# Two more matrix products of a hybrid decoder block as seven block products each

## The chip, the cores and the metric

The kernel runs on one core of one Trainium2 chip. The metric is the device time of one launch in microseconds. A core has a matrix engine (TensorE, "PE" in the profile; its weight loads are "PEld"), a vector engine (VectorE, "DVE"), an activation engine (ScalarE, "ACT"), a general engine (GpSimd, "POOL") and a queue engine (SyncE, "SP") that issues most of the transfers. Each engine executes its own instructions strictly in order. Operands lie in SBUF, results of PE in PSUM (eight banks of 128x512 float32).

## What is computed

One layer, for 1024 positions of width 1024, all in float32:

```python
u  = rmsnorm(h) ;  P = u @ W_in        # [gate_a | gate_s | B_a | C_a | v_a | z | xBC | dt]
y_a = (b_a * causal_dwconv(c_a * v_a, conv_a_w)) @ w_a_out            # 1024x1024 @ 1024x1024
y   = ssd_chunked_scan(...) + d_skip * xh                             # 32 heads, chunks of 128
y_s = gated_group_rmsnorm(y, z, ssd_norm_w) @ w_s_out                 # 1024x2048 @ 2048x1024
# gated_group_rmsnorm: y*silu(z), divided by the root mean square over groups of 512, times the weight
h  = h + (sigmoid(gate_a) * y_a + sigmoid(gate_s) * y_s) @ w_o
v  = rmsnorm(h)
h  = h + (silu(causal_dwconv(v @ W_1) + b) * (v @ W_3)) @ w_down      # d_ff 2816
out = rmsnorm(h)
```

## The kernel before

**Float32 products.** Every large product is made from rounded parts: a float32 tile is split into a high part (`act.copy` to float32r) and a low part (`split`, value minus high part, on DVE or POOL). A product of a 512x128 weight block and a 512x512 operand block is 12 matmuls with 512 moving columns: high x high, high x low and low x high, for four k-blocks each (`product`). In what follows "a product" is such a dozen.

**Seven block products.** The input projection, W_1 and W_3 already use seven products of half-size blocks where eight would be needed (the Strassen-Winograd form, class `Pair`): sums of operand blocks (`a11, a12, s1, s2, s4, s3, a22`) are formed and split once, sums of weight blocks per output pair. w_down does so too, with its weight sums (`w_sums`, a tensor `td` in DRAM) prepared beforehand. y_a, w_s_out and w_o are plain products.

**Order of the work.** (1) Input projection; beside it, from a counter of products (`tick`), the 32 SSD chunks (4 groups x 8) advance in steps at fixed offsets from the chunk's place, which are 6 products apart (`STAGES`, `ssd_chunk`). The last steps of a chunk multiply y by silu(z) (tile `zt`, 2 buffers), square it, store it to DRAM (`yd`, on ACT's queue), and get 1/rms of the 128 positions by a matmul with ones (`pn`), a multiply-add on DVE and a power on POOL; after every fourth chunk these are transposed (`pr`) and stored as a row (`rd`). (2) The y_a and w_s_out stage, for each half of the positions (`ta_half`, `y_a`, `y_half`, `s_out`): operands come from DRAM (`tad`, `yd`), y is multiplied by the norm weight and the row `rd` on DVE and split; for each of eight 128-wide output columns the weights are loaded, split (low part on DVE and POOL in turn) and multiplied, in both halves again. Outputs are gated on DVE; y_a's go through DRAM (`mad`). w_down's weight sums are made beside this stage, one k-block per output column. Then w_o (`out_proj`), for four row tiles at once in the first half and two in the second, with k-blocks 0 to 3 from the first four output columns and 4 to 7 from the others. (3) The MLP: 22 pairs of seven products, with the causal convolution and gating of each pair on ACT and DVE (`ffn_done`), sums of the gated result for w_down (`g_sums`), side tiles from a pool of two (`side`). (4) w_down in four sweeps, and the final norm.

A scheduler orders each engine's instructions before the run, by the program's order as priority and a simulated timeline; tiles come from pools with a fixed number of buffers (14 `big` ones of 128x2048, 4 `x` ones of the same size that exist only after the SSD, 13 weight parts `w`, 4 `raw` weight tiles), and whatever has no free buffer waits.

Of the kernel before, what the change touches and what calls it, by code (L numbers as in the profile page):

```python
# [8 lines left out]
F32 = mybir.dt.float32  # L9
# [44 lines left out]
STAGES = LOAD_M, LOAD_IN, DECAY, TRANS, LOAD_Z, DIAG, SQUARES, NORM = -9, -9, -6, -4, -3, 0, 3, 6  # L54
# [11 lines left out]
def tile_block(  # L66
# [633 lines left out]
    states, decayed, stats = {}, {}, {}  # L700

    def ssd_chunk(s):
# [104 lines left out]
        act.dma_start(yd[g, c // 4][:, :, hts], zt)  # L807
# [6 lines left out]
        rs = tiny(f"yss{nm}")  # L814
        dve.tensor_scalar(rs, pn, 1.0 / HALF, EPS, op0=ALU.mult, op1=ALU.add)
        if c % 4 == 0:
            stats[g, c // 4] = tiny(f"yr{nm}", 4)
        r = stats[g, c // 4]
        pool.tensor_tensor(r[:, c % 4 : c % 4 + 1], rs, nhalf, op=ALU.pow)
        if c % 4 == 3:  # L820

            pr = sd_tile(f"pr{nm}")[:4, :P]
            pe.transpose(pr, r, ident)
# [45 lines left out]
    def w_sums(k):  # L869

        r, r2 = (s4(f"wd{f}{k}")[:, :SEQ] for f in range(2))
        for f, t in enumerate((r, r2)):
            sp.dma_start(t, w_down[f * KF + k])
        b11, b12 = (r[:, h] for h in halves)
        b21, b22 = (r2[:, h] for h in halves)
        sub(b11, b12, b11)
        sub(b12, b22, b12, pool)
        sub(b22, b22, b11)
        sub(b21, b22, b21, pool)
        for i, t in enumerate((b11, b22, b12, b21)):  # L880
# [3 lines left out]
    def ta_half(hf, res):
        for q in range(2):
            new = extra_tile if hf and q else big_tile
            hi, lo = new(f"tah{hf}{q}", F32R), new(f"tal{hf}{q}", F32R)
            res.append((hi, lo))
            tt = (extra_tile if hf else big_tile)(f"ta{hf}{q}")
            for k in range(0, 4, 2):  # L890
                ks = slice(k, k + 2)
                sp.dma_start(tt[:, ks, :], tad[:, 4 * q + k : 4 * q + k + 2, halves[hf]])
                split(tt[:, ks, :], hi[:, ks, :], lo[:, ks, :], dve)
                yield

    def y_a(hf, ta, beside):
        sl = halves[hf]
        for j in range(NK):
            raw = load(w_a_out[j], f"wa{hf}{j}")
            ps = mm_tile(f"ya{hf}{j}")  # L900
            for q in range(2):
                w = wsplit(raw[:, halves[q]], f"wa{hf}{j}{q}", pool if q else dve)
                product(ps, ta[q], w, start=q == 0, stop=q == 1)
            gh = c2(f"ga{hf}{j}")
            sp.dma_start(gh, gad[:, j, sl])

            dve.scalar_tensor_tensor(gh, gh, 1.0, ps, op0=ALU.add, op1=ALU.mult)
            sp.dma_start(mad[:, j, sl], gh)
            beside(j)
# [448 lines left out]
```

## Time and profile before

| | |
|---|---|
| median of 3 runs | 1973.02 us (1971.64 to 1974.24) |
| profiled execution | 1974.46 us, span of its instructions 1972.7 us, granted clock 0.989 |
| PE, PEld | 1914.5 us busy (97%), 1572.0 (80%) |
| DVE, ACT, POOL | 1289.6 us (65%), 962.0 (49%), 1236.3 (63%) |
| chain that ended last | PE 80%, DVE 7%, ACT 4% |
| HBM | 247.34 MB read, 89.41 MB written |

The profile is one execution, taken by the hardware profiler. A row of groups reads: source line, engine, operation, output tile <- input tiles, shapes, count | busy us, mean ns of one | idle time before them and what ended it. A row of windows gives, for a stretch of the span, the busy time of each engine with its instruction count, then PE's granted clock, the share of the transfer engines and GB/s. A row of the chain of waits is start, duration, what. A row of the timeline is start, duration, engine, line, operation. An operation's duration includes time in which it is held up after its start. A matmul's own row says 389 ns, but matmuls overlap; their distance is read from the chain. Names: `ya` and `so` are the PSUM tiles of y_a and w_s_out, `l_x` and `h_x` low and high parts of a weight.

### The profile page before, as it was taken

How to read it: one execution, taken by the hardware profiler on the slowest of the kernel's cores; microseconds unless marked ns; L12 is line 12 of the kernel's file. 1: busy time of each engine (PE TensorE's matmuls, PEld its weight loads, DVE VectorE, ACT ScalarE, POOL GpSimd, SP SyncE). 2: the span in 40 equal slices, each digit the busy share in tenths (PEclk: the TensorE clock that was granted, in tenths of full speed). 3: DMA queues.
4: the chain of work that ended last, by engine and by line, in shares of the span. 5: the costliest groups of instructions: out<-in, count | busy, mean ns of one | idle time of the engine just before them, and what ended most of it. 6: DMA issues, size and time to landing. Idle time of an engine off the chain costs nothing.

```text
span 1972.7 us, 25409 instructions
## 1 busy us (share of the span) xinstructions
PE 1914.5 (97%) x8986; PEld 1572.0 (80%) x8986; DVE 1289.6 (65%) x1429; ACT 962.0 (49%) x1636; POOL 1236.3 (63%) x915
## 2 busy tenths in 40 slices
PE   7899999999999999999999999998999999999998
PEld 6678887787788778888888888876888888878886
DVE  8655567767776777777664833479854655585555
ACT  6345457677546664443542323354344444453334
POOL 6657776866776776676445533458876787845342
PEclk9899999999999999999999999998999999999999
DMA  4133355545445554443998974451323344487653
GB/s 166 54 111 121 122 164 172 162 150 190 155 133 164 164 164 124 146 157 110 382 376 279 356 250 161 161 170 35 136 80 108 101 150 163 139 285 264 206 188 143
DMA packets 180175, 338.42 MB, mean 172 GB/s; under 512 B 15280, under 2 KB 87760, under 8 KB 179024
## 3 DMA queue, kind: packets, MB, share of 16 engines
q1 hardware_dynamic: 93264, 253.95, 37.7%
q10 hardware_dynamic: 86784, 82.85, 13.1%
q8 instruction: 70, 1.15, 0.2%
q14 instruction: 57, 0.47, 0.1%
HBM read 247.34 MB, written 89.41 MB: 171 GB/s over the span
## 4 chain that ended last, share of the span: by engine, by line
PE 80%; DVE 7%; ACT 4%; issue 3%; DMA 3%; POOL 2%; ACTq 1%; SPq 0%; POOLq 0%; DVEq 0%
PE pb11up L268 10%; PE so L268 9%; PE pt1up L268 6%; PE pb11xb L268 5%; PE ya L268 4%; PE pb11cv L268 4%; PE d L1151 3%; PE d L1153 3%; PE d L1152 3%; PE pb11z L268 3%; PE pb21up L268 3%; PE pb11ba L268 2%; PE pt1cv L268 2%; PE pt1xb L268 2%; DMA m<-acd 2%
## 5 line engine op out<-in xcount | busy, mean ns | idle before, releaser
L608 DVE SCALAR_TENSOR_TENSOR cv<-xbc,scw,cv 128x1024 f32<-128x1024 f32 x72 | 122.6, 1704 | 46.3 <-ACT cv L604 45.0
L608 DVE SCALAR_TENSOR_TENSOR h<-fci,fcw,h 128x1024 f32<-128x1024 f32 x44 | 85.9, 1953 | 74.1 <-ACT h L604 73.3
L724 ACT ACTIVATE m<-m,tk 128x128 f32<-128x128 f32 x256 | 79.1, 390 | 95.3 <-DMA m<-acd 91.4
L149 POOL TENSOR_TENSOR l_ws<-raw_ws,h_ws 128x512 fp32r<-128x512 f32 x32 | 46.3, 1447 | 71.1 <-PE so L268 40.8
L148 ACT CAST h_ws<-raw_ws 128x512 fp32r<-128x512 f32 x64 | 39.9, 623 | 96.8 <-PE so L268 69.3
L268 PE MATMUL so<-yh,h_ws 128*128 128x512 f32 x256 | 69.0, 391 | 0.0
L268 PE MATMUL so<-yl,h_ws 128*128 128x512 f32 x256 | 68.6, 389 | 0.0
L268 PE MATMUL so<-yh,l_ws 128*128 128x512 f32 x256 | 68.5, 389 | 0.0
L148 ACT CAST h_wo<-raw_wo 128x512 fp32r<-128x512 f32 x48 | 29.7, 621 | 60.3 <-PE wo L985 32.7
L808 DVE TENSOR_TENSOR eb<-eb 128x256 f32<-128x256 f32 x32 | 28.1, 879 | 45.6 <-ACT eb L806 45.6
L149 DVE TENSOR_TENSOR l_ws<-raw_ws,h_ws 128x512 fp32r<-128x512 f32 x32 | 25.1, 785 | 50.0 <-PE so L268 25.5
L149 POOL TENSOR_TENSOR l_wo<-raw_wo,h_wo 128x512 fp32r<-128x512 f32 x24 | 32.3, 1346 | 39.1 <-PE wo L985 30.7
L268 PEld LDWEIGHTS so<-yh,l_ws 128*128 128x128 f32 x256 | 48.0, 188 | 10.0
L268 PEld LDWEIGHTS so<-yl,h_ws 128*128 128x128 f32 x256 | 48.0, 188 | 10.0
L268 PEld LDWEIGHTS so<-yh,h_ws 128*128 128x128 f32 x256 | 47.8, 188 | 9.7
L1128 DVE TENSOR_TENSOR h<-h 128x1024 f32<-128x1024 f32 x22 | 48.7, 2212 | 9.8 <-ACT h L1127 9.6
L314 DVE TENSOR_TENSOR fci<-fci,pb21up 128x512 f32<-128x512 f32 x18 | 12.4, 688 | 60.3 <-PE pb21up L268 60.3
L149 POOL TENSOR_TENSOR l_t3up<-raw_2up,h_t3up 128x512 fp32r<-128x512 f32 x22 | 30.3, 1376 | 32.7 <-PE pb11up L268 32.7
L984 PE MATMUL wo<-l_wo,mh 128*128 128x512 f32 x128 | 50.0, 391 | 0.0
L983 PE MATMUL wo<-h_wo,mh 128*128 128x512 f32 x128 | 49.9, 391 | 0.0
L985 PE MATMUL wo<-h_wo,ml 128*128 128x512 f32 x128 | 49.7, 391 | 0.0
L1127 ACT ACTIVATE h<-h 128x1024 f32<-128x1024 f32 x22 | 23.4, 1062 | 52.7 <-DVE h L608 52.7
(1125 smaller groups left out, 6571.8 us busy)
## 6 DMA issues: line engine op xcount, KB each, us to landing
m<-acd ACTq DMA_DIRECT2D x32, 512.0 KB, 3.9
raw_ws<-in_w_s_out SPq DMA_DIRECT2D x32, 512.0 KB, 4.7
ssd_in<-cv ACTq DMA_DIRECT2D x24, 512.0 KB, 3.1
in<-ssd_in ACTq DMA_DIRECT2D x32, 384.0 KB, 3.8
raw_wo<-in_w_o SPq DMA_DIRECT2D x24, 512.0 KB, 3.8
wd<-in_w_down SPq DMA_DIRECT2D x22, 512.0 KB, 7.0
td<-wd SPq DMA_DIRECT2D x44, 256.0 KB, 4.3
raw_2up<-in_w_up SPq DMA_DIRECT2D x22, 512.0 KB, 3.4
```

The lines of the kernel that those rows point to most:

```text
L148: act.copy(hi, v)
L149: (eng or pool).tensor_tensor(lo, v, f32(hi), op=ALU.subtract)
L268: pe.matmul(ps, wt[:, k, :], ct[:, k, :], start=(start and n == 0), stop=(stop and n == 11), skip_group_check=held,)
L608: dve.scalar_tensor_tensor(cv, ci[:, j : j + SEQ], w[:, j : j + 1], cv, op0=ALU.mult, op1=ALU.add)
L724: act.activation(m[:, h, :], m[:, h, :], AF.Relu, bias=a)
L983: pe.matmul(pss[t], mh, wh, start=k == 0, stop=False)
L984: pe.matmul(pss[t], mh, wl, start=False, stop=False)
L985: pe.matmul(pss[t], ml, wh, start=False, stop=k == NK - 1)
L1128: dve.tensor_tensor(cv, cv, h3, op=ALU.mult)
L1151: pe.matmul(ps, aa[0][:, ts], bb[0], start=k == 0, stop=False)
L1152: pe.matmul(ps, aa[0][:, ts], bb[1], start=False, stop=False)
L1153: pe.matmul(ps, aa[1][:, ts], bb[0], start=False, stop=k == KF - 1)
```

## The change

y_a and w_s_out are computed by one new function, `strassen`, over all 1024 positions and all 1024 output columns at once: the operand in four blocks (half of the positions x half of the k), the weights in four blocks, seven products per output column of the half (y_a 7x4x1 products of 12 matmuls, w_s_out 7x4x2). The sums over products are kept in PSUM banks across stages (`b1`, `b2`: four banks each) with two copies in SBUF (`x1`, `x2`).

- Operand sums are formed two stages ahead (`form`): blocks loaded from DRAM, sums on POOL in pieces of 128x1024, high part on ACT, low part on DVE. They use `big` tiles.
- Weight sums (`sums`) are made on DVE when a stage needs them. y_a's four weight blocks are loaded once and held; w_s_out's are loaded per stage, and two kinds of sums (stages s1, s2) are stored to DRAM and loaded again by later stages. All low parts of weights in these stages are on POOL.
- Outputs are finished in stages a12, s4 (first half of the positions) and s3, a22 (second half). w_o of the first half runs between s4 and s3; the norm and transposes of the first four row tiles run beside s3 and a22.
- y is normalised inside `ssd_chunk`: the 1/rms of 128 positions is put on a diagonal (DVE), multiplied by ones on PE (`pr`, now 128x128, every chunk), and y is scaled by it and the weight in four DVE operations, then stored. The row `rd`, its loads and the multiplications in `y_half` go. The steps are moved: `STAGES` has z's load one product later, the norm one earlier, and a new step SCALE at 7.
- w_down's weight sums (`w_sums`) move into `g_sums`, one k-block beside each of the first 11 pairs of the MLP, after that pair's gating, all four differences on DVE, with `side` tiles.
- `load_x` takes `big` tiles for the first half; `out_proj` finds the merged tiles by half.

```diff
-STAGES = LOAD_M, LOAD_IN, DECAY, TRANS, LOAD_Z, DIAG, SQUARES, NORM = -9, -9, -6, -4, -3, 0, 3, 6
+STAGES = LOAD_M, LOAD_IN, DECAY, TRANS, LOAD_Z, DIAG, SQUARES, NORM, SCALE = -9, -9, -6, -4, -2, 0, 3, 5, 7
...
         act.activation(sq, zt.rearrange("p j l -> p (j l)"), AF.Square)
-        act.dma_start(yd[g, c // 4][:, :, hts], zt)
...
-        pool.tensor_tensor(r[:, c % 4 : c % 4 + 1], rs, nhalf, op=ALU.pow)
-        if c % 4 == 3:
-            pr = sd_tile(f"pr{nm}")[:4, :P]
-            pe.transpose(pr, r, ident)
...
+        pool.tensor_tensor(r, r, nhalf, op=ALU.pow)
+        dve.tensor_scalar(sums, ident, r, None, op0=ALU.mult)
+        yield
+        pr = sd_tile(f"pr{nm}")[:, :P]
+        pe.matmul(pr, ones, sums, start=True, stop=True)
+        for j in range(4):
+            w = wns[:, 4 * g + j : 4 * g + j + 1]
+            dve.scalar_tensor_tensor(zt[:, j, :], zt[:, j, :], w, pr, op0=ALU.mult, op1=ALU.mult)
+        act.dma_start(yd[g, c // 4][:, :, hts], zt)
         yield
...
+    def strassen(name, nt, src, wsrc, done):
...
+        def form(c):
...
+                elif c == "s1":
+                    v, t = get(c, 1, 0, i), get(c, 1, 1, i)
+                    chain.append(v)
+                    for a, b in zip(parts(v), parts(t)):
+                        add(a, a, b, pool)
...
+                for n, a in enumerate(parts(v)):
+                    ks = slice(2 * n, 2 * n + 2)
+                    split(a, hi[:, ks, :], lo[:, ks, :], dve)
+                    yield
...
+        def sums(c, j):
+            pair = {
+                "a11": ((0, j),), "a12": ((1, j),), "s4": ((1, 4 + j),),
+                "s1": ((0, 4 + j), (0, j)), "s2": ((1, 4 + j), t1d),
+                "s3": ((1, 4 + j), (0, 4 + j)), "a22": ((1, j), t2d),
+            }[c]
...
+            if len(pair) == 2:
+                q = pair[1]
+                q = raw("q", q[j] if isinstance(q, list) else wsrc(*q))
+                sub(r, r, q)
+                if c in ("s1", "s2"):
+                    sp.dma_start((t1d if c == "s1" else t2d)[j], r)
+            return r
...
+        def run(c, beside):
+            for j in range(4):
+                if c == "a11":
+                    b1[j] = mm_tile(f"{name}b1{j}")
+                    prod(b1[j], c, j, True)
+                    act.copy(x1[:, j, :], b1[j])
+                elif c == "a12":
+                    p = sd_tile(f"{name}m2{j}")
+                    prod(p, c, j, True)
+                    done(0, j, x1[:, j, :], p)
...
+    ORDER = ("a11", "a12", "s1", "s2", "s4", "s3", "a22")
+    def gated(o, dr, hf, j, a, ps, nm):
+        g = c2(f"{nm}{hf}{j}")
+        sp.dma_start(g, dr[:, j, halves[hf]])
+        dve.tensor_tensor(o, a, ps, op=ALU.add)
+        dve.scalar_tensor_tensor(o, g, 1.0, o, op0=ALU.add, op1=ALU.mult)
...
+    run_stages(0, 12)
+    load_x(0)
+    out_proj(0, 4)
...
+    run_stages(12, 14, fill_beside)
...
+    def w_sums(k):
+        r, r2 = (side(f"wd{f}{k}", w_down[f * KF + k]) for f in range(2))
...
+    def g_sums(i, cv, free, after):
         a, b = (cv[:, h] for h in halves)
         if i < KF:
+            with tc.issue_after(after.ins):
+                w_sums(i)
```

More of the change, by code (lines that the diff above doesn't have):

```diff
@@ L884, in ta_half @@
[L884 to L909, printed above, removed]
@@ new lines, in tile_block, with ya_done, so_done @@
+    ORDER = ("a11", "a12", "s1", "s2", "s4", "s3", "a22")
[4 more added lines that the diff above has]
+        dve.scalar_tensor_tensor(o, g, 1.0, o, op0=ALU.add, op1=ALU.mult)
+    def ya_done(hf, j, a, ps):
+        o = c2(f"ya{hf}{j}")
+        gated(o, gad, hf, j, a, ps, "ga")
+        sp.dma_start(mad[:, j, halves[hf]], o)
+    mg = {}
+    def so_done(hf, j, a, ps):
+        q = j // 4
+        if (hf, q) not in mg:
+            new = extra_tile if hf == q else big_tile
+            mg[hf, q] = tuple(new(f"m{s}{hf}{q}", F32R) for s in "hl")
+        o, ma = c2(f"so{hf}{j}"), c2(f"ma{hf}{j}")
+        sp.dma_start(ma, mad[:, j, halves[hf]])
+        gated(o, gsd, hf, j, a, ps, "gs")
+        dve.tensor_tensor(o, o, ma, op=ALU.add)
+        hi, lo = mg[hf, q]
+        split(o, hi[:, j % 4, :], lo[:, j % 4, :])
@@ L1010, in v_norm, with run_stages, then_form, fill_beside @@
         return v
[L1012 to L1029 removed]
+    form_a, run_a = strassen(
+        "ya", 1, lambda hf, kh, i: tad[:, 4 * kh : 4 * kh + 4, halves[hf]],
+        lambda kh, j: w_a_out[NK * kh + j], ya_done,
+    )
+    form_s, run_s = strassen(
+        "so", 2, lambda hf, kh, i: yd[2 * kh + i, hf], lambda kh, j: w_s_out[NK * kh + j], so_done,
+    )
+    stages = [(form_a(c), run_a, c) for c in ORDER] + [(form_s(c), run_s, c) for c in ORDER]
+    def run_stages(n0, n1, beside=lambda n: None):
+        for n in range(n0, n1):
+            _, run, c = stages[n]
+            f = stages[n + 2][0] if n + 2 < len(stages) else iter(())
+            def then_form(j):
+                next(f, None)
+                beside(4 * (n - n0) + j)
+            run(c, then_form)
+            for _ in f:
+                pass
+    for n in range(2):
+        for _ in stages[n][0]:
+            pass
+    run_stages(0, 12)
     load_x(0)
[L1031 to L1035 removed]
+    out_proj(0, 4)
     V = operand("v")
[L1038 removed]
+    def fill_beside(n):
+        if n % 2 == 0:
+            fill_first(V, v_norm(n // 2), n // 2, f"v{n // 2}")
+    run_stages(12, 14, fill_beside)
     load_x(1)
```

195 lines of the change are left out of this document (99 added, 96 removed).

## The prediction

> **What bounds the kernel now.** I read the page first, then the table of windows, the chain of waits, the groups by shape, and last the timeline where two engines meet.
>
> ```profile
> span 1972.7 us, 25409 instructions
> PE 1914.5 (97%) x8986; PEld 1572.0 (80%) x8986; DVE 1289.6 (65%) x1429; ACT 962.0 (49%) x1636; POOL 1236.3 (63%) x915
> core 0: us, PE busy (x) PEld busy (x) DVE busy (x) ACT busy (x) POOL busy (x), PEclk, DMA share, GB/s
> 250.00:954.00 704.00, 691.18 (x3581) 562.99 (x3580) 518.18 (x610) 405.67 (x759) 492.66 (x374) 1.00 0.50 159
> 954.00:1003.00 49.00, 49.00 (x218) 40.58 (x217) 35.68 (x43) 22.76 (x32) 22.27 (x14) 1.00 1.03 405
> 954.00:1134.00 180.00, 180.00 (x792) 148.41 (x791) 119.03 (x137) 68.73 (x100) 89.85 (x58) 1.00 0.95 349
> 1134.00:1314.00 180.00, 180.00 (x817) 148.96 (x816) 77.85 (x109) 68.69 (x128) 71.93 (x57) 1.00 0.57 192
> 1314.00:1420.00 106.00, 95.13 (x401) 77.64 (x400) 96.24 (x86) 45.52 (x77) 91.95 (x61) 0.94 0.24 82
> 1420.00:1600.00 180.00, 180.00 (x796) 149.05 (x795) 97.11 (x89) 79.69 (x124) 128.00 (x97) 1.00 0.34 111
> ...
> 964.59 38.53 PE ya L268 x170
> 1003.12 87.04 PE so L268 x384
> ```
>
> PE is busy 97% of the span. The y_a and w_s_out stage with both out-projections lies from 954 to 1314 us, and there PE never rests: the chain is one unbroken run of its matmuls, 87.04 / 384 = 0.2267 us each, so a product of 12 takes 2.72 us. DVE and POOL look half idle there (119 and 90 of 180). The timeline, at places where the two meet, corrects that picture:
>
> ```profile
> 1447.42 1.29 POOL L149 TENSOR_TENSOR l_b11up<-raw_1up,h_b11up 128x512 fp32r<-128x512 f32 x1 [1.42 <-DMA raw_2up<-in_w_up]
> 1448.30 0.69 DVE L314 TENSOR_TENSOR fci<-fci,pb21up 128x512 f32<-128x512 f32 x1 [4.17 <-PE pb21up L268]
> ...
> 1360.67 1.72 POOL L326 TENSOR_TENSOR raw_1up<-raw_1up,t2up 128x512 f32<-128x512 f32 x1
> 1361.18 1.75 DVE L149 TENSOR_TENSOR vs2l<-h,vs2h 128x512 fp32r<-128x512 f32 x1
> 1362.35 1.72 POOL L149 TENSOR_TENSOR l_t2up<-t2up,h_t2up 128x512 fp32r<-128x512 f32 x1
> 1362.86 1.76 DVE L250 TENSOR_TENSOR a12v<-a12v,h 128x512 f32<-128x512 f32 x1
> 1364.03 1.73 POOL L149 TENSOR_TENSOR l_t3up<-raw_2up,h_t3up 128x512 fp32r<-128x512 f32 x1
> ...
> 1373.11 4.35 DVE L608 SCALAR_TENSOR_TENSOR h<-fci,fcw,h 128x1024 f32<-128x1024 f32 x2 [0.43 <-ACT h L604]
> 1374.11 2.27 POOL L325 TENSOR_TENSOR raw_2up<-raw_2up 128x512 f32<-128x512 f32 x1
> 1376.34 2.28 POOL L326 TENSOR_TENSOR fx<-fx,t2up 128x512 f32<-128x512 f32 x1
> ...
> L651 DVE SCALAR_TENSOR_TENSOR cc<-pr,caw,cc x16: 1272/1283/2358, 555.7 to 915.0; 128x1024 f32<-128x1024 f32 x16
> ```
>
> A POOL operation takes 1.29 us and a DVE operation with one operand in PSUM 0.69 us, even side by side (first two rows). When the DVE operation reads two SBUF tiles, both stretch to about 1.74 us and each engine starts one every 1.68 us: they take turns. Beside DVE operations twice as wide POOL starts one every 2.23 us, so 512 more elements on DVE cost 0.55 us. I therefore count turns: DVE 0.55 us (128x512) or 1.10 (128x1024), POOL 1.68 - 0.55 = 1.13 (128x512), and, no wider POOL operation being in the trace, 2.26 as an estimate for 128x1024. DVE and POOL together are one resource for this kind of work.
>
> The Trainium skill states this as a rule (SBUF — State Buffer, Who interferes with whom): a DVE instruction with two SBUF inputs and a GpSimd instruction that reads SBUF exclude each other for a whole instruction. The rows agree in kind: 1.68 us for the two is close to one after the other. What whole lengths would make of the time is priced among the rivals.
>
> **The change, part by part.**
>
> *Fewer products.* y_a goes from 32 products to 28, w_s_out from 64 to 56: 144 matmuls less x 0.2267 = **-32.6 us** on PE, which is the path. y_a is then 28 x 2.72 = 76.2 us of PE, w_s_out 56 x 2.72 = 152.3, that is 21.8 for one of its stages.
>
> *What the products now ask of DVE and POOL.* Sums of blocks and splits of the operands are two-SBUF work. y_a: 28 weight splits on POOL 31.6 us, 8 operand sums 128x1024 on POOL 18.1, 14 operand splits on DVE 15.4, 16 weight differences 8.8, 16 gatings 8.8: 82.7 us of turns beside 76.2 of PE. w_s_out: 56 weight splits 63.3, 16 operand sums 36.2, 16 low parts of the merged result 18.1, 28 operand splits 30.8, 16 weight differences (128x1024) 17.6, 32 gatings and additions 17.6: 183.6 beside 152.3. (The additions of a product in PSUM take no turn.) The split of two operands and the first six weight pairs (13 buffers) can be ready when y_a begins: 11.2 us. The worst point is the start of stage s4 of w_s_out. Needed by then: y_a 82.7; stages a11 to s2 with their operands, 32 weight splits 36.2, 8 differences 8.8, 16 operand splits 17.6, 8 sums 18.1, 4 outputs 8.9; and the operand of s4 with a first weight 14.5: 186.8 - 11.2 = 175.6, against 76.2 + 4 x 21.8 = 163.4 of PE. PE is short by 12.2. The operand of s3 (13.4), formed early by the program's order, may add to it, although the out-projection after s4 (43.5 us of PE, 13.4 of turns) leaves room for it later. I take **+14**, bounds 0 (the MLP below feeds PE fully) and 40 (nothing overlaps).
>
> *The end of a22.* The second out-projection takes its k-blocks 2 and 3 after 12 matmuls, 2.7 us, and block 3 is the last output of a22. Its addition, gating, addition, cast and low part are long beside that:
>
> ```profile
> L149 POOL TENSOR_TENSOR ml<-gs,mh 128x512 fp32r<-128x512 f32 x16 | 24.4, 1527 | 26.4 <-ACT mh L148 26.4
> L951 DVE TENSOR_TENSOR gs<-gs,ma 128x512 f32<-128x512 f32 x16 | 14.3, 896 | 0.4
> L148 ACT CAST mh<-gs 128x512 fp32r<-128x512 f32 x16 | 10.0, 622 | 15.3 <-DVE gs L951 15.3
> L950 DVE SCALAR_TENSOR_TENSOR gs<-gs,so 128x512 f32<-128x512 f32 x16 | 11.0, 685 | 25.1 <-PE so L268 22.7 <-issue 2.3
> ```
>
> 0.69 + 0.90 + 0.90 + 0.62 + 1.53 = 4.6, and the four tiles of the norm's V stand in the same queues: **+3** (1.9 to 8).
>
> *Normalising beside the SSD.* Per chunk one fp32 product of 128x128 more, and a scaling of five small DVE operations.
>
> ```profile
> 260.52 0.22 PE pc L734 x2
> 360.77 0.27 PE pr L823
> PE pr L823 <- POOL yr L819: 2.8, 3, 2.3
> L751 DVE TENSOR_TENSOR cb<-pc,tri 128x128 f32<-128x128 f32 x32 | 8.9, 278 | 0.0
> L926 DVE SCALAR_TENSOR_TENSOR y<-y,wns,rb 128x512 f32<-128x512 f32 x32 | 25.9, 868 | 7.0 <-DMA rb<-rd 4.0 <-DMA y<-yd 3.0
> ```
>
> The product is of the kind of `pc`: 32 x 0.22 = 7.0 on PE, less eight transposes `pr` of 0.27, 2.2: +4.8. DVE: 5 x 0.278 x 32 = 44 us more on 518 of 704 (74% to 80%); with one operand in PSUM they take no turn. The old `pr` waited for POOL's power 2.8 us in all, 0.35 per transpose. The new one waits for pn, DVE, POOL and DVE again, 32 times, but is placed two ticks later (5.4 us and more): between -2.8 (never waits) and 32 x 0.35 - 2.8 = +8.4; I take +3, nearer to never, since most old ones did not wait. Together **+8** (2 to 13). The store of y now waits on ACT's queue for the scaling; casts and exponentials stand behind it, ACT is busy 406 of 704, and z's buffer is refilled three ticks after the store (six before): within the +8. The 32 multiplications of L926 (25.9 us) and the 8 row loads go; nothing waited for them while PE was full: 0.
>
> *w_down's sums beside the MLP.* 44 DVE differences of 128x512; 22 loads and 44 stores move on SP's queue past the loads of w_up. A pair takes 7 x 2.72 = 19.0 us and 9 POOL turns (10.2), three wide DVE turns and three narrow ones (4.95): 15.1, 80%. Four more make 17.3, 91%: still hidden from 1420 us on, where PE is full today. From 1314 to 1420 DVE is busy 96 of 106, and the first three sets (6.6 us of turns) fall near its end: **+1.5** (0 to 7). In the old place nothing is gained by their leaving but the turns counted above. A store waiting for its difference holds w_up's loads behind it; four raw buffers cover that.
>
> *Transfers.* In stages s1 and s2 each w_s_out column moves two loads and a store of 512 KB, and the next operand 2 MB: 8.4 MB in 21.8 us, 385 GB/s. From 954 to 1003 us the queues carried 405 GB/s with a share of 1.03 and PE did not stop. Taken as 0 (up to 10).
>
> Sum: -32.6 + 14 + 3 + 8 + 1.5 = -6.1. The profiled execution took 1974.46 us (span 1972.7 and 1.8 around it), 1.4 above the median 1973.02: 1974.5 - 6.1 - 1.4 = **1967 us**.
>
> **The rivals.**
>
> *The shared turns do not bind* (operands and weights arrive in time, as PE is kept full from 1420 to 1600 with POOL busy 128 and DVE 97 of 180): without 14 and with half the rest, -32.6 + 6 = 1946. For it: turns there are only 80%; against it: here they are 109 and 121% of PE's time.
>
> *All of it is eaten.* Stalls of 29 to 36 us, each term near its upper middle: 1969 to 1977, no change.
>
> *The other side: turns bind harder.* Place: s1, s2 and s4 of w_s_out. Queues in order put the next stage's operand sums (4 x 2.26) in front of the current weights. It decides the sign once PE waits over 20 us in that stage (32.6 - 8 - 3 - 1.5); with the operand of s3 ahead as well, 12.2 + 13.4 = 26, plus a few us of slower clock, it gives 1981 to 1990. If each turn cost the whole length that the operation has alone (0.69 us on DVE, 1.27 for 128x1024 by the shortest of the last row above, 1.29 on POOL, 2.58 for the wide one), the same sum before s4 gives about 204 us of turns for the work counted as 175.6, a stall of 40, and 1993. Against whole lengths: the pair that takes 1.68 us and not 1.98. What speaks for a clock price is this window, with PE waiting for DVE's splits:
>
> ```profile
> 1345.00:1366.00 21.00, 14.02 (x48) 10.71 (x47) 21.00 (x16) 7.63 (x14) 18.85 (x12) 0.85 0.00 0
> PE pt1up L268 <- DVE vs1l L149: 3.9, 1, 3.9
> ```
>
> The granted clock fell to 0.85 there. The Trainium skill (TensorE: Matmul & The Clock Gate, What's actually happening) has the clock halved after about 3.4 us of idling; the wait of 3.9 us agrees. Shorter waits, as I expect them, would cost nothing more by it.
>
> *The new product in the SSD waits for every chunk*, 0.35 to 0.7 us: +16 to +27 instead of 8, with the rest as summed 1976 to 1986. Against it: 5.4 us of distance; for it: two more hops of busy DVE.
>
> **How the numbers follow.** Likeliest: part of the saving is eaten, 1953 to 1969, 0.36. The turns do not bind: 0.12. All is eaten: 0.20. Turns bind harder: 0.22. The SSD's product waits: 0.10. 0.2%, about what a measurement of this kernel can tell from no change, is 3.9 us: faster 0.36 + 0.12 = 0.48, same 0.20, slower 0.32. The range 1946 to 1991 reaches to the ends of the cases and leaves out half of the second and a fringe of the slow ones.
>
> **What would show it.** In the profile after: `ya` and `so` with 336 and 672 matmuls; POOL and DVE both near full from y_a to s4, with weight splits and operand splits of 1.7 us and longer; PE waiting there for `l_` weights (POOL) or operand splits (DVE), 10 to 20 us in all; `pr` with 64 matmul records and waits of a few us; the MLP's pairs still 19.0 us apart. The forecast is wrong if PE has no waits between y_a and s4 (then 1946), if those waits pass 20 us, if `pr` waits in most chunks, or if the MLP's pairs stretch while w_down's sums run.

## The result, and the profile after

The changed kernel takes 2020.66 us (median, 2016.88 to 2025.02) against 1973.51 before (1971.64 to 1974.24) on the same chip: ratio 1.0241 [1.0219, 1.0264], **47 us slower**. The forecast was 1967 us, with a range from 1946 to 1991. The profiled execution took 2016.88 us, its span is 2015.1, 42.4 more than before (it is the shortest of its runs, so the medians lie 5 us further apart).

The head of the page after, and the table of windows by stage (SSD; y_a; w_s_out to the start of the first out-projection; the rest to the MLP; the MLP's first 106 us; the MLP at its pace):

```profile
span 2015.1 us, 25406 instructions
PE 1911.5 (95%) x8898; PEld 1549.7 (77%) x8898; DVE 1451.8 (72%) x1621; ACT 972.1 (48%) x1648; POOL 1355.0 (67%) x953
core 0: us, PE busy (x) PEld busy (x) DVE busy (x) ACT busy (x) POOL busy (x), PEclk, DMA share, GB/s
250.00:977.00 727.00, 707.89 (x3645) 566.78 (x3644) 546.04 (x768) 404.71 (x751) 487.26 (x375) 1.00 0.49 156
977.00:1071.00 94.00, 84.24 (x348) 67.81 (x347) 83.56 (x64) 41.26 (x60) 74.85 (x37) 0.95 0.60 208
1071.00:1197.00 126.00, 113.47 (x482) 89.97 (x480) 80.64 (x51) 42.82 (x64) 112.14 (x57) 0.99 0.70 249
1197.00:1350.00 153.00, 142.08 (x623) 114.61 (x623) 101.48 (x121) 65.04 (x124) 78.88 (x57) 0.98 0.68 235
1350.00:1456.00 106.00, 91.97 (x374) 73.83 (x373) 98.91 (x90) 43.08 (x73) 85.52 (x57) 0.92 0.32 112
1456.00:1636.00 180.00, 179.63 (x791) 148.09 (x791) 150.18 (x124) 78.88 (x123) 144.09 (x96) 1.00 0.59 203
```

PE executes what was announced: 8986 - 144 + 56 (64 records of `pr` instead of 8) = 8898. Where it was full before (180.00 of 180.00 in the y_a rows of the prediction) it now has gaps and the transfers have room. DVE and POOL are near full at y_a (83.56 and 74.85 of 94), POOL at w_s_out (112 of 126).

Three places lost time. Each starts or ends at a first or last product, read from the views of the tiles:

| | before | after | difference | prediction |
|---|---|---|---|---|
| last start in tile `pb11g`, the input projection's last product but one (here called the end of the SSD) | 961.5 | 977.8 | +16.3 | +8 |
| from there to the MLP's first product (1314.6; 1350.4) | 353.1 | 372.6 | +19.5 | -32.6 + 14 + 3 = -15.6 |
| from there to the MLP's last `pb11up` (1758.7; 1801.5) | 444.1 | 451.1 | +7.0 | +1.5 |

Together 42.8, the growth of the span within 0.4.

The second row is the surprise. The timeline in y_a after, some rows of it, shows how it goes:

```profile
1007.07 6.08 POOL L861 TENSOR_TENSOR yas<-yas,yas 128x1024 f32<-128x1024 f32 x2
...
1008.12 2.84 DVE L1008 SCALAR_TENSOR_TENSOR ya<-ga,ya 128x512 f32<-128x512 f32 x1
...
1010.88 2.82 DVE L861 TENSOR_TENSOR yaw<-yaw,yaw 128x512 f32<-128x512 f32 x1
1013.63 0.68 DVE L1007 TENSOR_TENSOR ya<-yax,yam 128x512 f32<-128x512 f32 x1
1014.23 0.68 DVE L861 TENSOR_TENSOR yaw<-yaw,yaw 128x512 f32<-128x512 f32 x1
...
1014.46 2.04 PE L268 MATMUL yab<-yas1h,h_yas 128*128 128x512 f32 x4 [5.59 <-DVE ya L1007]
...
1015.00 0.62 ACT L148 CAST h_yas<-yaw 128x512 fp32r<-128x512 f32 x1 [13.33 <-DVE yaw L861]
```

POOL forms two operand sums of 128x1024. Beside them two DVE operations of 128x512 take 2.84 and 2.82 us (the second starts 2.76 us after the first), where the same weight difference takes 0.68 a little later, at 1014.23. The addition that frees PE's PSUM bank (L1007, 0.68 us, one operand in PSUM) is itself not held up, but it stands behind those two in DVE's queue: PE waits 5.59 us. The weight difference of L861 is late too, and ACT's cast waits 13.33 us for it. The longest waits of PE in the whole region (total, times, longest), where before there was no wait at all:

```profile
PE yab L268 <- DVE ya L1007: 9.6, 4, 5.6
PE sob L268 <- ACT h_sos L148: 6.5, 4, 2.6
PE sob L268 <- POOL l_sos L149: 5.3, 5, 1.6
PE pt_v L187 <- DVE h L1083: 5.0, 2, 4.2
PE wo L1057 <- ACT mh L148: 2.0, 1, 2.0
```

### The profile page after: what moved, and what is told of

Read it like the earlier page. It is cut to its first block, busy times and chain, and to the rows that moved or that the text cites. A ratio compares the mean times of both kernels' runs of the same rounds, so it can differ in the third digit from the quotient of the medians.

```text
span 2015.1 us, 25406 instructions
## 1 busy us (share of the span) xinstructions
PE 1911.5 (95%) x8898; PEld 1549.7 (77%) x8898; DVE 1451.8 (72%) x1621; ACT 972.1 (48%) x1648; POOL 1355.0 (67%) x953
## 5 line engine op out<-in xcount | busy, mean ns | idle before, releaser
L797 POOL TENSOR_TENSOR sn<-st,cdb 128x512 f32<-128x512 f32 x24 | 36.8, 1534 | 47.3 <-DVE st L792 37.3
L816 DVE TENSOR_SCALAR ss<-ident,yr 128x128 f32<-128x128 f32 x32 | 27.3, 852 | 53.6 <-POOL yr L814 51.7
L149 POOL TENSOR_TENSOR l_wo<-raw_wo,h_wo 128x512 fp32r<-128x512 f32 x24 | 37.3, 1556 | 25.6 <-PE wo L1059 18.9
L751 DVE TENSOR_TENSOR m<-m,cb 128x1024 f32<-128x1024 f32 x32 | 51.6, 1613 | 0.5
L149 POOL TENSOR_TENSOR l_t3xb<-raw_2xb,h_t3xb 128x512 fp32r<-128x512 f32 x12 | 19.8, 1654 | 35.8 <-ACT h_t3xb L148 21.1
L614 ACT ACTIVATE cv<-cv 128x1024 f32<-128x1024 f32 x24 | 25.5, 1061 | 36.1 <-DVE cv L607 35.9
L323 POOL TENSOR_TENSOR raw_1up<-raw_2up,raw_1up 128x512 f32<-128x512 f32 x20 | 29.1, 1455 | 20.1 <-DMA raw_2up<-in_w_up 17.7
L149 POOL TENSOR_TENSOR l_t4up<-raw_1up,h_t4up 128x512 fp32r<-128x512 f32 x20 | 42.0, 2098 | 0.0
L744 POOL TENSOR_TENSOR in<-in,dsk 128x512 f32<-128x512 f32 x32 | 38.3, 1196 | 0.9 <-PE px L729 0.9
L822 DVE SCALAR_TENSOR_TENSOR zt<-zt,wns,pr 128x128 f32<-128x128 f32 x128 | 35.6, 338 | 3.8 <-PE pr L819 3.8
L814 POOL TENSOR_TENSOR yr<-yr,nhalf 128x1 f32<-128x1 f32 x32 | 23.1, 723 | 22.6 <-DVE yr L813 22.6
L861 POOL TENSOR_TENSOR h<-h,gk 128x512 f32<-128x512 f32 x11 | 19.0, 1724 | 26.5 <-DVE gk L861 25.2
```

The lines of the kernel that those rows point to most:

```text
L149: (eng or pool).tensor_tensor(lo, v, f32(hi), op=ALU.subtract)
L751: dve.tensor_tensor(m, m, cb.unsqueeze(1).to_broadcast([P, HG, P]), op=ALU.mult)
```

## The experiments

Lengths of stages below run from the first product of a stage to that of the next. "Start of s4" is the time from y_a's first product to the first of w_s_out's stage s4, the point for which the prediction made its sum; without stalls it is 163.4 us. In the changed kernel it is 201.6 us, in y_a and then in w_s_out:

```profile
971.80:1070.70 98.90, 89.14 (x361) 71.64 (x362) 83.95 (x65) 43.14 (x63) 79.56 (x41) 0.93 0.62 218
1070.70:1173.40 102.70, 91.46 (x385) 72.20 (x384) 68.33 (x43) 34.97 (x53) 88.98 (x46) 0.98 0.75 268
```

PE runs 744 matmuls there (each row counts those at its edges) and not 720: 24 of the input projection fall in between, 5.4 us. At 0.2267 us the 744 take 168.7. PE stands idle for 201.6 - 89.14 - 91.46 = 21.0 us, and the other 11.9 are matmuls that run slower. By the granted clock in the two rows about 0.07 x 98.9 + 0.02 x 102.7 = 9 us of these are clock: behind the wait of 5.59 us four matmuls take 2.04 us, where four take 1.07 in the stretch ahead of the waits. So 5.4 of the 38.2 us over 163.4 are no loss, and 32.8 are.

**The parts, one by one.** The kernel before with the normalised y alone, and with w_down's sums alone.

```diff
# e1_ssd_only, from before: STAGES, ssd_chunk and y_half as in the change; y_a, w_s_out, w_down as before
# e2_wd_only, from before: w_sums moved into g_sums as in the change; nothing else
```

> The kernel before with one part of the change: y normalised inside the SSD's steps (the new product pr, the diagonal and four scalings on DVE, the moved steps), and the multiplications by the row taken out of the y_a and w_s_out stage. Theory A (the SSD pays by itself: the DVE operation that writes the diagonal waits for POOL's power, 51.7 us in 28 waits in the changed kernel's SSD, and what is queued on DVE behind it comes late): +10 to +17 us against the kernel before, about 1985 to 1990, with DVE's waits for yr again near 50 us, and the stage from y_a to the MLP as long as before (353 us). Rival B (the SSD's 16 us come from what the next stage asks for early, as the operands of y_a are loaded and split beside the last chunks): no change beyond the product's own time, 0 to +5 us.

> The kernel before with one other part of the change alone: w_down's sums beside the first 11 pairs of the MLP instead of beside y_a and w_s_out. Theory A (turns of DVE and POOL on SBUF: the MLP's start is already full, and 44 more DVE operations there cost PE time): +4 to +8 us against the kernel before, with the first pairs of the MLP stretched and the later ones 19.0 us apart; nothing gained from 954 to 1314 us, where PE was never idle. Rival B (the MLP's start is late in the changed kernel only because the stage ahead delivers its last tiles late): 0 to +2 us.

Measured: 1992.08 us, 1.0095 [1.008, 1.011], for the first; the SSD ends at 977.7 as in the changed kernel, and the region behind it still takes 353.1. And 1980.33 us, 1.0035 [1.0022, 1.0048], for the second; from the MLP's first product to its last `pb11up` 449.9 us instead of 444.1. Both parts lose by themselves, by 19 and 7 us. Theory A held for the second (+4 to +8). For the first rival B falls; Theory A's place and its waits for `yr` are there (51.3 us), but the loss passes its range of 10 to 17, and how much of it those waits make is taken up below. The windows of the second kernel show where it loses (the MLP's first 106 us, and then its pace):

```profile
1314.00:1420.00 106.00, 90.21 (x373) 72.13 (x373) 99.11 (x89) 43.17 (x73) 85.10 (x57) 0.94 0.32 112
1420.00:1600.00 180.00, 179.63 (x791) 148.07 (x790) 147.33 (x125) 79.84 (x123) 143.81 (x97) 1.00 0.60 203
```

Against the rows of before in the prediction PE loses 95.13 - 90.21 = 4.9 us in the first stretch, where DVE goes from 96.24 to 99.11 of 106, and 0.4 in the second.

**Region: are POOL's operand sums the cost?** The changed kernel without them; with them on DVE; and, as a check on the first, with POOL kept as long in writes that read nothing.

```diff
# e4_no_opsums (all four kinds of sums in form())
-                    for a, b in zip(parts(v), parts(t)):
-                        add(a, a, b, pool)
...
# e7_opsums_dve
-                        add(a, a, b, pool)
+                        add(a, a, b)
...
# e12_sums_as_memsets
-                        add(a, a, b, pool)
+                        pool.memset(a, 0.5)
+                        pool.memset(a, 0.5)
+                        pool.memset(a[:, 0, :], 0.5)
...
```

> The changed kernel without the 24 x 2 operations of 128x1024 on POOL that form the sums of operand blocks (the blocks are still loaded, split and multiplied, so the products are of other values). Theory A (the turns that DVE and POOL take on SBUF bound the y_a and w_s_out stage): 24 operations of y_a and w_s_out in pieces, about 54 us of turns, go, the sum falls under PE's time, and the stage shortens by 30 to 45 us, total 1975 to 1990. Rival B (weights come late: two loads, a store and a reload per column in s1, s2 and a22): at most 10 us faster, 2010 or more. Rival C (operand tiles come late for lack of free buffers): at most 15 us faster, 2005 or more, as all the tiles are still there.

> The changed kernel with the 24 operand sums of 128x1024 on DVE instead of POOL, all else as it is. Theory A (one resource; 2.28 us of it from POOL by the changed kernel's rows, 1.10 from DVE, and the short DVE operations no longer wait 2.28 us for each of them): 24 x 1.18 = 28 us of turns go, and the kernel gets 10 to 28 us faster, 1992 to 2010. Rival B (DVE's own queue): 24 x 1.2 = 29 us more for an engine that is full at the start of the stage, 5 to 25 us slower, 2025 to 2045.

> The changed kernel with each of POOL's 24 operand sums of 128x1024 replaced by writes of a constant into the same tile at the same place, 128x1024 twice and 128x512 once, about 2.3 us on POOL, as long as a sum takes there alone. So POOL is as busy as in the changed kernel, its weights' low parts stand behind the same queue, but the writes read nothing; in the measurement by itself a DVE addition beside such writes ran at its own 0.60 us. Theory A (the turns with DVE are what the sums cost): near the run without the sums, 1985 to 1995, w_s_out's stages s1 and s2 near 21.8 us each. Rival B (POOL's own time in its queue is what they cost, the weights' low parts being late): near the changed kernel, 2012 to 2022, s1 and s2 still 27 to 32.

| | time, ratio to before | start of s4 | over 163.4 | of it PE idle, slower matmuls | stages s1, s2 |
|---|---|---|---|---|---|
| after | 2020.66, 1.0241 [1.0219, 1.0264] | 201.6 | 38.2 | 21.0, 11.9 | 31.6, 27.6 |
| operand sums on DVE | 2002.77, 1.0149 [1.0134, 1.0164] | 191.6 | 28.2 | 13.2, 9.7 | 26.4, 25.5 |
| POOL writes instead of sums | 1993.7, 1.0105 [1.0085, 1.0124] | 178.6 | 15.2 | 6.7, 3.2 | 21.7, 24.2 |
| no operand sums | 1987.05, 1.0071 [1.0052, 1.0091] | 174.5 | 11.1 | 4.6, 1.2 | 21.8, 21.7 |

(In the first of these expectations "24 x 2" should read 24; there are 24 sums in all.) The view of tile `sob` in the changed kernel, in the one with POOL's writes and in the one without sums, carries the last column (first and last start of a stage's h x h matmuls). The 24 matmuls of the input projection are in every row, 5.4 us of the fourth column.

```profile
L268 PE MATMUL sob<-sos1h,h_sos x32: 389/389/504, 1114.2 to 1141.0; 128*128 128x512 f32 x32
L268 PE MATMUL sob<-sos2h,h_sos x32: 387/389/500, 1145.8 to 1171.4; 128*128 128x512 f32 x32
L268 PE MATMUL sob<-sos4h,h_sos x32: 389/389/393, 1173.4 to 1194.7; 128*128 128x512 f32 x32
```

```profile
L268 PE MATMUL sob<-sos1h,h_sos x32: 389/389/389, 1107.6 to 1127.3; 128*128 128x512 f32 x32
L268 PE MATMUL sob<-sos2h,h_sos x32: 389/389/497, 1129.3 to 1151.5; 128*128 128x512 f32 x32
L268 PE MATMUL sob<-sos4h,h_sos x32: 389/389/389, 1153.5 to 1173.2; 128*128 128x512 f32 x32
```

```profile
L268 PE MATMUL sob<-sos1h,h_sos x32: 389/389/389, 1106.6 to 1126.3; 128*128 128x512 f32 x32
L268 PE MATMUL sob<-sos2h,h_sos x32: 389/389/389, 1128.4 to 1148.1; 128*128 128x512 f32 x32
L268 PE MATMUL sob<-sos4h,h_sos x32: 389/389/389, 1150.1 to 1169.8; 128*128 128x512 f32 x32
```

Theory A held in all three (with POOL's writes s2 still takes 24.2, not 21.8). Taking the sums away returns 27.1 of the 32.8 us that are lost. Writing for as long on POOL's queue costs back only 4.1 of them. So most of it is not POOL's time but the reading beside DVE. One difference was not separated: the writes are three short operations where a sum is one, and weights' low parts run between them. With the sums on DVE 10 us come back before s4, and 17.9 in the whole.

**The turns by themselves.** A kernel that computes nothing of the layer: rows of additions on resident tiles, on DVE and POOL.

```diff
# e9_turn_bench: for each pair of kinds, n operations on each engine, then a DVE copy that waits for both
+    seg(d_two, 16, 512, p_two, 16, 1024)    # both read two SBUF tiles
+    seg(d_two, 16, 512, p_two, 16, 512)
+    seg(d_two, 16, 1024, p_two, 16, 1024)
+    seg(d_two, 16, 128, p_two, 16, 1024)
+    seg(d_psum, 40, 512, p_two, 16, 1024)   # DVE's second operand in PSUM
+    seg(d_one, 40, 512, p_two, 16, 1024)    # DVE tensor_scalar, one operand
+    seg(d_two, 40, 512, p_set, 24, 1024)    # POOL only writes
```

> This kernel computes nothing of the layer: it only runs rows of additions on DVE and POOL, alone and side by side, on resident tiles. Theory A (the turns of the prediction, but handed over one for one): alone, POOL takes about 2.4 us for 128x1024 and 1.2 for 128x512, DVE about 0.6 and 1.2 with two SBUF inputs. Side by side each pair of one DVE and one POOL operation takes 0.55 + 2.26 = 2.8 us (512 beside 1024), 1.68 (512 beside 512), 3.4 (1024 beside 1024), and a DVE operation of only 128x128 beside POOL's 128x1024 still comes once per POOL operation, every 2.4 us or so: 16 of them take about 39 us. A DVE operation with its second input in PSUM, or with one input, stays at 0.6 to 0.7 us beside POOL, and a DVE addition beside POOL's memsets stays at about 0.6. Rival B (turns are shared out by time, not by count, as the prediction's sum assumed): in the same four pairs the DVE operations are through before POOL's, several between two POOL operations: the 16 of 128x128 in less than 10 us. Rival C (no turns, only bandwidth): DVE stretches by less than 1.5 times beside POOL in every pair, and a PSUM operand or a memset makes no difference.

Its timeline, the rows of the segments (start, duration of all, x count):

```profile
9.84 27.59 POOL L42 TENSOR_TENSOR po<-p,q 128x1024 f32<-128x1024 f32 x12 [5.49 <-DVE q L50]
37.98 15.11 POOL L42 TENSOR_TENSOR po<-p,q 128x512 f32<-128x512 f32 x12 [0.55 <-DVE q L50]
...
54.31 5.50 DVE L33 TENSOR_TENSOR do<-a,b 128x512 f32<-128x512 f32 x9
61.33 12.57 DVE L33 TENSOR_TENSOR do<-a,b 128x1024 f32<-128x1024 f32 x11
74.89 39.12 DVE L33 TENSOR_TENSOR do<-a,b 128x512 f32<-128x512 f32 x15
122.13 6.10 DVE L33 TENSOR_TENSOR do<-a,b 128x512 f32<-128x512 f32 x10
122.36 26.24 POOL L42 TENSOR_TENSOR po<-p,q 128x512 f32<-128x512 f32 x16 [3.86 <-DVE q L50]
149.92 43.84 DVE L33 TENSOR_TENSOR do<-a,b 128x1024 f32<-128x1024 f32 x14
200.66 0.28 DVE L33 TENSOR_TENSOR do<-a,b 128x128 f32<-128x128 f32 x1
200.93 30.99 DVE L33 TENSOR_TENSOR do<-a,b 128x128 f32<-128x128 f32 x15
201.17 37.56 POOL L42 TENSOR_TENSOR po<-p,q 128x1024 f32<-128x1024 f32 x16 [0.62 <-DVE q L50]
239.51 21.01 DVE L36 TENSOR_TENSOR do<-a,ps 128x512 f32<-128x512 f32 x35
276.85 0.42 DVE L39 TENSOR_SCALAR do<-a 128x512 f32<-128x512 f32 x1
277.26 47.47 DVE L39 TENSOR_SCALAR do<-a 128x512 f32<-128x512 f32 x39
327.04 22.36 DVE L33 TENSOR_TENSOR do<-a,b 128x512 f32<-128x512 f32 x37
```

Alone: POOL 27.59 / 12 = 2.30 us and 15.11 / 12 = 1.26, DVE 0.61, 1.14 and 0.28. Beside POOL's 128x1024 the rows give 39.12 / 15 = 2.6 us for a DVE operation of 128x512, 3.1 for 128x1024 and 30.99 / 15 = 2.07 for 128x128, but in each the first one or two ran before POOL had begun. From there on one starts every 2.75, 3.28 and 2.35 us, once per POOL operation. Less what they take from start to start alone (0.60, 1.14, 0.20) that is 2.14 to 2.15 each time: the DVE operation pays one whole POOL operation, however short it is, and its own length on top. With the second operand in PSUM (21.01 / 35 = 0.60), or beside writes (22.36 / 37 = 0.60), nothing is paid. Theory A holds in these (in its four pairs it had 2.8, 1.68, 3.4 and 2.4); rivals B and C fall. Two rows are not as it said. `tensor_scalar` with a single SBUF operand pays too: the sixteen that run beside POOL's sixteen additions start every 2.48 us, the others of the 39 every 0.34. And in the pair of two 128x512 the ten DVE operations ran at 0.61 us while POOL's first one waited: 16 x 1.26 + 6.1 = 26.2, POOL's whole stretch. There DVE kept the turn. What decides who gives way stays open.

**Region: transfers, and the low parts.**

```diff
# e5_no_t_store (s2 and a22 subtract a loaded block instead of the stored sum)
-                q = raw("q", q[j] if isinstance(q, list) else wsrc(*q))
+                q = raw("q", wsrc(0, j) if isinstance(q, list) else wsrc(*q))
-                if c in ("s1", "s2"):
-                    sp.dma_start((t1d if c == "s1" else t2d)[j], r)
# e6_lo_dve (half of the weights' low parts on DVE)
-                wsplit(r[...], f"{name}{c}{j}{i}") for i in range(nt)
+                wsplit(r[...], f"{name}{c}{j}{i}", dve if i or (nt == 1 and j % 2) else pool) for i in range(nt)
```

> The changed kernel without the store and reload of weight sums in w_s_out: stages s2 and a22 subtract the plain block (0, j) instead of the stored sum (other values), the number of loads stays, 8 stores of 512 KB go, and nobody waits for a store to land. Theory A (turns of DVE and POOL bound the stage): at most 8 us faster than the changed kernel, 2012 to 2021. Rival B (transfers bound s1, s2 and a22; DVE waited 11.5 us there for a reloaded sum): 10 to 20 us faster, 2000 to 2010.

> The changed kernel with half of the low parts of weights in y_a and w_s_out on DVE instead of POOL (14 and 28 of them), all else as it is. DVE is the busier engine where the stage begins (47.0 of 47 us from 1003 to 1050). Theory A (one resource, on which such an operation costs 0.55 us from DVE and 1.13 from POOL): 42 x 0.58 = 24 us of turns go, and the kernel gets 8 to 25 us faster, 1995 to 2012. Rival B (DVE's own queue is what PE waits for; PE's longest waits there are for a DVE addition, 9.6 us): 5 to 20 us slower, 2025 to 2040.

Measured: 2021.7 us, 1.0244 [1.0229, 1.0259], and 2021.9, 1.0247 [1.0225, 1.0269]; neither differs from the changed kernel. For the first, Theory A held: the stores and the wait for them cost nothing, as predicted (the loads stayed, so this run says nothing of them). The low parts on DVE gave neither theory's number: w_s_out's s1 went from 31.6 to 27.1 and s4 with the out-projection from 73.1 to 69.0, but y_a, where DVE is the fuller engine, went from 98.9 to 106.0.

**The SSD.** Two versions of the changed kernel first, with the diagonal on POOL, and with diagonal and scaling a step later each.

```diff
# e3_diag_pool
-        dve.tensor_scalar(sums, ident, r, None, op0=ALU.mult)
+        pool.tensor_scalar(sums, ident, r, None, op0=ALU.mult)
# e8_diag_late
-... SQUARES, NORM, SCALE = -9, -9, -6, -4, -2, 0, 3, 5, 7
+... SQUARES, NORM, WRITE, SCALE = -9, -9, -6, -4, -2, 0, 3, 4, 7, 8
         pool.tensor_tensor(r, r, nhalf, op=ALU.pow)
+        yield
         dve.tensor_scalar(sums, ident, r, None, op0=ALU.mult)
```

> The changed kernel with the diagonal of 1/rms written by POOL, right behind its own power, instead of by DVE. Theory A (DVE stands still behind the diagonal, and the SSD's 16 us are that): 8 to 14 us faster than the changed kernel, about 2005 to 2012, with DVE's waits for yr gone. Rival B (the SSD's 16 us are the new product's time on PE and the four scalings on DVE): within 3 us of the changed kernel, 2017 to 2022.

> The changed kernel with the SSD's last steps apart: squares at 3, the product pn and the power at 4 (5 before), the diagonal on DVE only at 7 (at 5 before), the new product and the scalings at 8 (7 before). Theory A (DVE stands still behind POOL's power because the diagonal follows it at once): DVE's waits for yr fall from 51.7 us to under 20, and the SSD ends 6 to 12 us earlier, total 2008 to 2015. Rival B (what counts is the product's PE time and one more late step on a full DVE or POOL, as with the diagonal on POOL, which ended 5 us later): within 4 us of the changed kernel.

Measured: 2021.73, 1.025 [1.0223, 1.0277], the SSD's end at 983.1; and 2032.9, 1.0303 [1.0286, 1.032], its end at 979.3. Both theories that expected a gain fell. Rival B's number held in the first (within 3 us), and fell in the second, which is 12 us slower than the changed kernel and not within 4. (In its profiled execution 1.5 us of the loss lie before the end of the SSD and 7 between there and the MLP; that was not followed up.) In the first, DVE's wait for the power is gone, and PE's product waits for POOL instead:

```profile
PE pr L819 <- POOL ss L816: 11.1, 6, 5.5
```

In the second DVE still stands for the power, 57.5 us in all against 51.7:

```profile
DVE ss L816 <- POOL yr L814: 57.5, 26, 4.9
```

Then from the side of before: one thing added at a time, or one taken from e1.

```diff
# e10_product_only, from before: a product that waits for nothing and that nobody reads
         pe.matmul(pn, sums, ones[:, :1], start=True, stop=True)
+        px = sd_tile(f"px{nm}")[:, :P]
+        pe.matmul(px, ones, sums, start=True, stop=True)
# e11_no_scaling, from e1_ssd_only
-        for j in range(4):
-            w = wns[:, 4 * g + j : 4 * g + j + 1]
-            dve.scalar_tensor_tensor(zt[:, j, :], zt[:, j, :], w, pr, op0=ALU.mult, op1=ALU.mult)
# e13_moved_steps, from before: STAGES as in the change, y stored in the step SCALE
# e14_no_wait_for_power, from e1_ssd_only
-        dve.tensor_scalar(sums, ident, r, None, op0=ALU.mult)
+        dve.tensor_scalar(sums, ident, wns[:, :1], None, op0=ALU.mult)
```

> The kernel before, with one more fp32 product of 128x128 (ones by the sums of squares) behind `pn` in each of the 32 chunks; its operands are ready when `pn` has run, and nothing reads its result. So it costs PE's own time and no wait. Theory A (the product itself costs about 0.25 us on PE, 0.14 for its columns and 0.11 for the change of format back, and the other half of the SSD's 16 us are waits of its chain): 6 to 10 us slower than before, about 1981, all of it before 961.5 + 8. Theory B (all of the 16 us are waits and late DVE work): 0 to 3 us slower. Theory C (all of it is PE's time and the clock): 14 to 18 us slower.

> The kernel before with y normalised beside the SSD as in the change, but without the four scalings of each chunk on DVE (y is stored as it was squared; the product `pr` is made and not read). Theory A (the chain pn, multiply-add, power, diagonal, `pr`, with DVE standing for POOL's power, and the product's own time make the cost): still 14 to 19 us slower than before, about 1988 to 1992. Theory B (the 36 us of scalings make DVE's other work in the chunks late): 6 to 11 us slower, near the extra product alone.

> The kernel before with only the order of the steps changed as in the change: z's load one product later, the norm one earlier, and the store of y in a step of its own at 7. The row of 1/rms, its transposes and the later multiplication stay as before; there is no new product, no diagonal and no scaling. Theory A (the moved steps, z's buffers held longer and ACT's queue make the SSD longer): 8 to 15 us slower than before. Theory B (DVE standing for POOL's power is the cost): 0 to 3 us slower.

> The kernel before with y normalised beside the SSD as in the change, except that the diagonal is made with a constant column instead of the power's result. All operations stay (the multiply-add, POOL's power, the diagonal, the product, the four scalings), and so do the moved steps; only DVE's wait for POOL in front of the diagonal goes, and y is scaled by the constant. Theory A (the moved steps are the cost): still 14 to 20 us slower than before. Theory B (DVE standing for POOL's power is the cost): 3 to 8 us slower, the extra product and little more, and `pr` without waits.

| | time, ratio to before | end of the SSD, against before | PE busy, idle from 250 us to there |
|---|---|---|---|
| before | 1973.02 | 961.5 | 698.7, 12.8 |
| extra product alone | 1976.02, 1.0018 [1.0008, 1.0027] | 963.7, +2.2 | 706.1, 7.6 |
| moved steps alone | 1976.6, 1.0022 [1.0013, 1.0032] | 963.5, +2.0 | 701.5, 12.0 |
| all but the wait for the power | 1986.87, 1.0072 [1.0055, 1.0088] | 971.4, +9.9 | 708.9, 12.5 |
| all (e1) | 1992.08, 1.0095 [1.008, 1.011] | 977.7, +16.2 | 710.1, 17.6 |
| all but the scalings | 1993.47, 1.012 [1.0094, 1.0146] | 979.3, +17.8 | 711.6, 17.7 |

The end of the SSD is read from tile `pb11g`; in the kernel before, in the extra product alone, and in all but the wait:

```profile
L268 PE MATMUL pb11g<-ua22h,l_t4g x20: 388/389/473, 366.6 to 961.5; 128*128 128x512 f32 x20
```

```profile
L268 PE MATMUL pb11g<-ua22h,l_t4g x20: 389/389/481, 367.8 to 963.7; 128*128 128x512 f32 x20
```

```profile
L268 PE MATMUL pb11g<-ua22h,l_t4g x20: 389/389/390, 371.3 to 971.4; 128*128 128x512 f32 x20
```

Of 16.2 us the product alone is 2.2, the moved steps alone 2.0, DVE's wait for the power 16.2 - 9.9 = 6.3 (by the medians 18.9 - 14.2 = 4.7). The scalings are nothing: without them it is no faster. The other 5.7 are not any part's own. The last column, of one execution each, shows where they may lie: the extra product keeps PE busy for 7.4 us more, 0.23 each, and delays it by only 2.2 because PE stands idle 5.2 us less. With all but the wait PE is busy 10.2 us more, about what the product (7.4) and the moved steps (2.8) add, and its idle time does not fall; with the wait it is idle 5.1 us more again. Why the idle time falls beside the product alone and not beside all parts was not tested. Against the expectations: the product's total is in Theory B's range, but its cost on PE is the 0.25 of Theory A; the version without scalings goes to "the chain" (Theory A), a little past its range. Of the last two runs neither theory holds: the moved steps alone cost 4 us and not 8 to 15, and without the wait 14 us remain and not 3 to 8. No single part makes the cost. The groups and waits of the changed kernel show what the diagonal costs DVE:

```profile
L816 DVE TENSOR_SCALAR ss<-ident,yr 128x128 f32<-128x128 f32 x32 | 27.3, 852 | 53.6 <-POOL yr L814 51.7 <-POOL fci L1141 1.7
L814 POOL TENSOR_TENSOR yr<-yr,nhalf 128x1 f32<-128x1 f32 x32 | 23.1, 723 | 22.6 <-DVE yr L813 22.6
L822 DVE SCALAR_TENSOR_TENSOR zt<-zt,wns,pr 128x128 f32<-128x128 f32 x128 | 35.6, 338 | 3.8 <-PE pr L819 3.8
```

One operation of 128x128 takes 0.85 us in the mean (it is a `tensor_scalar`, the kind that pays turns in the separate measurement), and DVE stands idle 1.6 us in front of each: 27.3 + 53.6 = 81 us of DVE's queue for 32 small operations. The power takes 0.72 us on POOL for 128 numbers. PE's named waits for `pr` are only 5.5 us in all, and PE's idle time in the SSD grows from 12.8 to 19.1 us: most of the time that DVE stands does not reach PE as idle time.

## Why the prediction was wrong, step by step

**-32.6 of products: right.** The 144 matmuls are gone; without stalls, the sum by stages holds (w_s_out's a11 and a12 take 21.7 and 21.8).

**The shared turns, +14 with bounds 0 to 40: the step that failed.** The turns were named, their sizes were right (2.26 + 0.55 = 2.81 was predicted for a pair of 128x1024 and 128x512; the trace has 2.76 from one start to the next, the separate measurement 2.75), and the place was right in part. Before s4 PE loses 32.8 us instead of 12.2: 21.0 idle and 11.9 in slower matmuls. What failed first is the addition of all turns into one resource that serves whatever is due. DVE has to go through its queue in order and gets about one operation for each of POOL's, however short its own is: in y_a every gating and weight difference that falls beside an operand sum pays 2.15 us more, and the additions that free PSUM stand behind. So one engine's queue is late while the sum of turns still has room: at the prediction's prices the operations that ran between y_a's first product and that of s4 (on POOL 66 of 128x512 and 20 of 128x1024, on DVE 40 and 38) are about 184 us of turns in 201.6. y_a alone loses 98.9 - 76.2 - 5.4 = 17.3 us, a place to which the prediction gave no stall. In w_s_out it is POOL that is late: PE waits there for `h_sos` and `l_sos`, and DVE itself stands 11.9 us for one weight that is loaded late. That the order in the queues is the reason is read from these rows; no run changed the order alone.

What failed second is the clock, put at a few us in a rival and at nothing in the sum. The prediction expected waits shorter than 3.9 us and no clock lost behind them. The measurement differs: ahead of 1003.36 PE waited 2.94 us and the granted clock from 1003 to 1008 is 0.66; ahead of 1145.77 it waited 2.59 us, and from 1145 to 1151 it is 0.72.

The rival "whole lengths" had 204 us and a stall of 40, close to 201.6 and 38.2, but by luck: a pair takes 2.75 us, not 0.61 + 2.30 = 2.91, and 3.28, not 3.44; 5.4 of the 38.2 are other products, and 11.9 are slower matmuls. After s4 two more stages are long (s4 with the out-projection 73.1 for 65.3, s3 28.6 for 21.8); from y_a's first product to the MLP it makes 378.6 - (360.6 - 32.6) = 50.6 against 14 + 3. The Trainium skill (SBUF — State Buffer, Who interferes with whom) states the exclusion for two SBUF inputs; the measurement agrees, with 2.75 against 0.60 us from start to start.

**The end of a22, +3 (1.9 to 8): the size is right by PE's waits.** At that place they are 2.0 us for `mh`, 0.4 for the gated output and 0.8 for V's tiles, 3.2 in all; no run separated them. V's tiles cost PE 4.2 us at another place, in stage s3, and the first out-projection waits 2.2 us for its own weights; the sum had neither. They are part of the 50.6.

**Normalising beside the SSD, +8 (2 to 13): mis-sized.** 16.3, outside its range. The product's 7.0 us on PE were right (PE is busy 7.4 us more), though alone it delays the SSD by only 2.2. The waits were put at +3; DVE's wait for the power alone makes 6.3. The moved steps, taken as within the +8 for the store on ACT's queue and z's buffer, are 2.0 alone. What the parts cost together beyond that, 5.7, stays open. The step counted how long PE waits for `pr` by the old transposes, and took the four DVE operations of a chunk at 0.278 us each and the diagonal too (0.34 and 0.85 in the trace). It didn't count that DVE itself stands in front of the diagonal, 51.7 us in all, with everything else of the chunk behind it. "What is queued behind the waiting instruction" was asked of ACT's queue and not of DVE's.

**w_down's sums, +1.5 (0 to 7): at the upper bound.** 5.8 alone, 7.0 in the changed kernel. Hidden from 1420 us on, as said (179.63 of 180). But DVE had 10 us free in the MLP's first 106 us, and the sets laid there cost PE 4.9: a DVE that is busy for 91% of a stretch had no room for them.

**Transfers, 0: not contradicted** (2021.7 without the stores; without the operand sums, with every load still in place, s1 and s2 take 21.8 and 21.7 us).

Sum by the runs: 16.3 + 19.5 + 7.0 = 42.8 instead of -6.1. Of the rivals, "turns bind harder" had a right place, s1 and s2 of w_s_out, and a right reason, the queues in order, but nothing for y_a and too little clock; it was combined with the SSD's and the MLP's terms at their likeliest values, and both came out at or over their upper ends, so 1991 was too low.

No version run here beats the kernel before: even without any operand sum (1987.05) the 15.3 us that the region gains (337.8 for 353.1) are less than what the SSD and the MLP give back.

## What to carry to other kernels

When matrix products are saved by sums of operands, cost the sums by each engine's queue in order, and let every DVE operation that reads only SBUF beside POOL's wide ones pay a whole POOL operation on top of its own length; then look for what PE needs that stands behind it, and price the clock that PE loses after the waits. Where an instruction of a busy engine waits for a small result of another one, look at all that is queued behind it, and then test what of it reaches PE: here DVE stood 51.3 us, and taking the wait away gave back 6.3. Work that is moved beside a stage is hidden only if the engines are free at the time it arrives there, not in the stage's mean.

## What the hardware showed that was not expected

- A DVE addition of 128x128, 0.28 us alone, comes every 2.35 us beside POOL's additions of 128x1024; one with an operand in PSUM keeps its 0.60 us, and so does any DVE addition beside POOL's writes of constants.
- `tensor_scalar` with one float32 operand in SBUF pays as well: every 2.48 us beside POOL's additions, every 0.34 after them.
- In one pair (both 128x512) DVE held the turn for ten operations, 6.1 us, and POOL waited. Turns are not always one for one.
- After PE had waited 2.59 us the granted clock was 0.72 over the next 6 us.
- 32 extra float32 products of 128x128 among the large ones keep PE busy for 7.4 us more, 0.23 each, and delay the end of the stretch by 2.2, as PE's idle time there falls by 5.2 us.
